# Long convolution of 1024 tokens: eight residues of 128 in place of four of 256, with the larger butterfly on VectorE

## The chip, the cores and the metric

One core of one Trainium2 chip runs the whole program. The metric is device time in microseconds; three runs of the kernel before gave 2500.44, 2504.18 and 2507.24, median 2504.18.

## The reference, cut to what matters

One encoder layer is applied to two groups with shared weights: "sample" (1024 tokens, group 0 in the kernel) and "prompt" (512 tokens, group 1). The part that changes is the Hyena branch's bidirectional long convolution over the sequence, for 512 channels:

```python
def bidir_long_conv(v, h_f, h_b):
    L = v.shape[1]
    k = concatenate([h_f, zeros, h_b[1:][::-1]])          # filter of length 2L
    return irfft(rfft(v, 2 * L) * rfft(k, 2 * L), 2 * L)[:, :L]
y = bidir_long_conv(v, h_f, h_b) + v * fbias
```

`h_f`, `h_b` come out of a small sine MLP, times a decaying window, divided by the sum of absolute values. After it come the branch projections, gates, an output projection, and a squared-ReLU MLP: `x + gt2 * (square(relu(h2 @ w_ff1)) @ w_ff2)`. All in float32; the kernel writes each operand of a matmul as a high and a low part (`fp32r`) and sums three products.

## The kernel before, in words

**Transform.** The convolution is done by matmuls against cosine and sine tables at odd frequencies, in groups ("units") of 128 channels, four units for each group of tokens. The sequence of length L is split into four residues (token index modulo 4) of L/4 each, so the sample has residues of 256 and the prompt of 128. `filter_spectrum` (L504) makes eight tap blocks with two matmuls of 256 columns each (L515 to L540), then the spectrum: for each of two frequency halves `j`, 24 matmuls of 128 columns for the even residues (L564, L565) and 24 of 256 columns for the odd ones (L578, L580), all through `dft_mm` (L496), combined on VectorE and stored to DRAM (`d_b`). `long_conv` (L598) transposes the input (L621), runs for each half `j` 24 matmuls of 256 columns (L634), a four-point butterfly, the product with the spectrum and the inverse butterfly on VectorE (L645 to L679), transposes back (L691), and at the end 48 matmuls of 256 columns to token order (L721). The tables are streamed from DRAM on POOL's queue, 1 MB at a time, into the ring `cst` (three buffers in the spectrum, two in the convolution; L485 to L494): ten loads of `k_fs` and four of `k_gs` for each unit.

**Order.** Spectrum and convolution of the sample are generators that run beside the main work: `run(main, bg, ratio)` (L1421) emits `ratio` steps of the background for each step of the main generator. For the sample (L1576 to L1595) the main work is the prompt's branch projections (8 steps, ratio 1), its output projection (8, ratio 1), one step of the sample's gate products, and the prompt's MLP `ffn` (L1027; 64 steps, ratio 2.0). Each `ffn` step is 24 matmuls of 512 columns, for one weight block of 512 KB that SP's queue loads and that is split into high and low parts on ACT (L196) and VectorE (L198). The "up" steps evacuate through ACT (relu, square) and VectorE (L1035 to L1039), the last of every four "down" steps through VectorE (`gated_add`, L971 and L972). The builder's scheduler then places instructions on each engine; it may put an instruction that is ready ahead of one emitted earlier. Engines run their instructions in that fixed order.

**After it.** `load_y` (L1594, L901) reads the convolved sample from `d_y` and splits it (L889, L890) for the sample's branch projections, which begin at once (L1627). PSUM has two banks for the background (`bg`) and four for the main matmuls in this stretch.

Of the kernel before, what the change touches and what calls it, by code (L numbers as in the profile page):

```python
# [12 lines left out]
F32 = mybir.dt.float32  # L13
# [8 lines left out]
P = 128  # L22
# [28 lines left out]

def _row_order(L):
    q = L // 4
    return np.concatenate([4 * np.arange(q) + r for r in range(4)])


def _constants():
# [15 lines left out]
    for L, tag in zip(LENS, "sp"):  # L73
        J = L // 4
        nj, nu = J // P, J // P
        om = math.pi * (np.arange(J) + 0.5) / L
        F = np.zeros((nj, P, 6, nu, 2, P))
        G = np.zeros((4, P, nj, 2, J))
        for r in range(4):
            ang = np.outer(om, 4.0 * np.arange(J) + r)  # L80
            for cs, fn in enumerate((np.cos, np.sin)):
                m = fn(ang)
                f = m.reshape(nj, P, nu, P).transpose(0, 3, 2, 1)
                slot = (r // 2) if r % 2 == 0 else 2 + r // 2
                F[:, :, slot, :, cs, :] = f
                if r % 2 == 1:
                    F[:, :, 4 + r // 2, :, cs, :] = -f if cs else f
                G[r, :, :, cs, :] = m.reshape(nj, P, J).transpose(1, 0, 2)
        c["k_f" + tag] = np.stack(_hilo(F), 3)
        c["k_g" + tag] = np.stack(_hilo(G), 2)  # L90
    i = np.arange(P)
    ms = [i[:, None] == i[None]]
# [17 lines left out]
def encoder_trunk(ctx: ExitStack, tc: tile.TileContext, a: dict, dbg=None):  # L110
# [374 lines left out]
    def load_f(pool, g, j, s0, bufs):  # L485
        t = pool.tile([P, 2, 2, n_of[g] // 512, 2, P], F32R, name="cst", bufs=bufs)
        G.dma_start(t, a["k_f" + tags[g]][j][:, s0:s0 + 2])
        return t

    def load_g(pool, g, r0, nb, bufs):  # L490
        n = n_of[g]
        t = pool.tile([P, nb, 2, n // 512, 2, n // 4], F32R, name="cst", bufs=bufs)
        G.dma_start(t, a["k_g" + tags[g]][r0:r0 + nb].rearrange("r p h j s u -> p r h j s u"))
        return t  # L494
# [9 lines left out]
    def filter_spectrum(g, u, h3, wo, pool):  # L504
        n = n_of[g]
        nu = n // 512
# [3 lines left out]
        F = load_f(pool, g, 0, 0, 3)  # L510
        pm = {}
        for r in range(4):
            for ut in range(nu):
                i = r * nu + ut
                ps = psum("bg")[:, 0:2 * P]  # L515
                T.matmul(ps, lhsT=h3[:, i * P:(i + 1) * P], rhs=wo[0][:, :, c0:c0 + P], start=True, stop=False)
                T.matmul(ps, lhsT=h3[:, i * P:(i + 1) * P], rhs=wo[1][:, :, c0:c0 + P], start=False, stop=True)
                win = pool.tile([P, P], F32, name="kwin", bufs=3)
                nc.sync.dma_start(win, a["k_win"][row0 + i * P:row0 + (i + 1) * P, c0:c0 + P])
                hw = pool.tile([P, 2, P], F32, name="khw", bufs=2)  # L520
                V.tensor_tensor(hw, ps.rearrange("p (d c) -> p d c", d=2),
                                win[:, None, :].broadcast_to([P, 2, P]), op=ALU.mult)
                hw2 = hw.rearrange("p d c -> p (d c)")
                if i == 0:
                    V.memset(hw[0:1, 1, :], 0.0)
                    S.activation(acc, hw2, AF.Abs)
                else:
                    ab = pool.tile([P, 2 * P], F32, name="kab", bufs=1)
                    S.activation(ab, hw2, AF.Abs)
                    V.tensor_tensor(acc, acc, ab, op=ALU.add)  # L530
                f = pool.tile([P, 2, P], F32, name="kpm", bufs=2)
                V.tensor_tensor(f[:, 0, :], hw[:, 0, :], hw[:, 1, :], op=ALU.add)
                s = (1, 0) if r == 3 else (0, 1)
                V.tensor_tensor(f[:, 1, :], hw[:, s[0], :], hw[:, s[1], :], op=ALU.subtract)
                fh = pool.tile([P, 2, P], F32R, name=f"kh{i}", bufs=1)
                S.copy(fh, f)
                fl = pool.tile([P, 2, P], F32R, name=f"kl{i}", bufs=1)
                V.tensor_tensor(fl, f, fh.bitcast(F32), op=ALU.subtract)
                pm[r, ut] = (fh, fl)
                yield  # L540
# [5 lines left out]
        V.reciprocal(nsc[:, g * 4 + u:g * 4 + u + 1], tmp)  # L546

        def terms(F, lst, cs):
            res = []
            for r, d, slot in lst:  # L550
                for ut in range(nu):
                    fh, fl = pm[r, ut]
                    res.append((fh[:, d, :], fl[:, d, :], F[:, slot, 0, ut, cs, :], F[:, slot, 1, ut, cs, :]))
            return res
# [3 lines left out]
        for j in range(n // 512):  # L558
            Fo = load_f(pool, g, j, 2, 3)
            Fn = load_f(pool, g, j, 4, 3)  # L560
            eb = []
            for r in (0, 2):
                ps = psum("bg")[:, 0:2 * P]
                dft_mm(ps[:, lo], terms(F, [(r, 0, r // 2)], C))  # L564
                dft_mm(ps[:, hi], terms(F, [(r, 1, r // 2)], Sn))  # L565
                eb.append(ps)
            s0 = pool.tile([P, 2 * P], F32, name="ks0", bufs=1)
            S.copy(s0, eb[0])
            e0 = pool.tile([P, 2 * P], F32, name="ke0", bufs=1)
            e1 = pool.tile([P, 2 * P], F32, name="ke1", bufs=1)  # L570
            V.tensor_tensor(e0, s0, eb[1], op=ALU.add)
            V.tensor_tensor(e1, s0, eb[1], op=ALU.subtract)
            if (j + 1) * 512 < n:
                F = load_f(pool, g, j + 1, 0, 3)
            yield
            yield
            pp = psum("bg")[:, 0:2 * P]
            dft_mm(pp, terms(Fo, [(1, 0, 0)], CS) + terms(Fn, [(3, 0, 1)], CS))  # L578
            mm = psum("bg")[:, 0:2 * P]
            dft_mm(mm, terms(Fn, [(1, 1, 0)], CS) + terms(Fo, [(3, 1, 1)], CS))  # L580
            Bt = pool.tile([P, 4, 2 * P], F32, name="kB", bufs=1)
            V.tensor_tensor(Bt[:, 0, lo], e0[:, lo], pp[:, lo], op=ALU.add)
            V.tensor_tensor(Bt[:, 2, lo], e0[:, lo], pp[:, lo], op=ALU.subtract)
            V.tensor_tensor(Bt[:, 1, lo], e1[:, lo], pp[:, hi], op=ALU.subtract)
            V.tensor_tensor(Bt[:, 3, lo], e1[:, lo], pp[:, hi], op=ALU.add)
            V.tensor_tensor(Bt[:, 0, hi], e0[:, hi], mm[:, hi], op=ALU.subtract)
            V.tensor_tensor(Bt[:, 2, hi], e0[:, hi], mm[:, hi], op=ALU.add)
            V.tensor_tensor(Bt[:, 1, hi], e1[:, hi], mm[:, lo], op=ALU.add)
            V.tensor_tensor(Bt[:, 3, hi], e1[:, hi], mm[:, lo], op=ALU.subtract)
            G.dma_start(d_b[g][u][j], Bt)  # L590
            yield
# [6 lines left out]
    def long_conv(g, u, pool, vx, ahead):  # L598
        n = n_of[g]
        nu = nj = n // 512  # L600
        J = n // 4
# [6 lines left out]
        def load_b(j):  # L608
            t = wt()
            nc.sync.dma_start(t, d_b[g][u][j])  # L610
            return t

        Fe = load_f(pool, g, 0, 0, 2)
        Bt = load_b(0)
        yield
        yield
        v = {}
        for r in range(4):
            ps = psum("bg")
            for ut in range(nu):  # L620
                T.transpose(ps[:, ut * P:(ut + 1) * P], _ap(vx, 4 * ut * P + r, [[4, P]]), ident)  # L621
            vh = pool.tile([P, nu, P], F32R, name=f"lvh{r}", bufs=1)
            pv = ps[:, 0:nu * P].rearrange("p (u c) -> p u c", u=nu)
            S.copy(vh, pv)
            vl = pool.tile([P, nu, P], F32R, name=f"lvl{r}", bufs=1)
            V.tensor_tensor(vl, pv, vh.bitcast(F32), op=ALU.subtract)
            for ut in range(nu):
                v[r, ut] = (vh[:, ut, :], vl[:, ut, :])
        Fo = load_f(pool, g, 0, 2, 2)
        yield  # L630

        def fwd(F, r):
            ps = psum("bg")[:, 0:w2]
            dft_mm(ps, [v[r, ut] + (F[:, r // 2, 0, ut, :, :], F[:, r // 2, 1, ut, :, :]) for ut in range(nu)])  # L634
            return ps

        nb = 1 if J == 256 else 4
        Q = []
        for j in range(nj):
            At = wt()  # L640
            tmp = wt()
            b0 = fwd(Fe, 0)
            S.copy(tmp[:, 0, :], b0)
# [1065 lines left out]
```

## Time and profile before

| | |
|---|---|
| median of 3 runs | 2504.18 us |
| profiled execution | 2507.51 us |
| its span, first to last instruction | 2505.7 us |
| mean granted TensorE clock (share of 2.4 GHz) | 0.989 |
| PE / PEld / DVE / ACT busy | 2445.6 / 2003.5 / 1722.4 / 996.1 us |
| POOL's DMA queue (q0), moved | 161.91 MB |

PE is the matmul engine, PEld its weight loads, DVE is VectorE, ACT is ScalarE, POOL is GpSimd, SP only issues DMAs. Matmuls are pipelined: a record covers a matmul's whole way through the array, so the cost of one in a stream is the distance from its start to the next start, not the length of its record. Idle times of an engine come with the instruction that ended them.

### The profile page before, as it was taken

To read this page: it belongs to the slowest core of one execution; us is meant where nothing else is said; L and a number is where in the kernel's file an instruction comes from. 1 tells how busy PE (TensorE), PEld (TensorE's weight loads), DVE (VectorE), ACT (ScalarE), POOL (GpSimd) and SP (SyncE) were. 2 spreads that over 40 slices of the span, in tenths; PEclk is the share of its full clock that TensorE was granted. 3 is DMA by queue.
4 is the path that set the end of the run, shared out by engine and by line. 5 is a ranking of instruction groups with operands and counts; after the bars stand their busy time and mean duration, and the time that the engine had idled before them with its cause. 6 is when DMAs were issued, how large, how long until landed. Compare 5 with 4: busy or idle time off the path is not lost.

```text
span 2505.7 us, 32508 instructions
## 1 busy us (share of the span) xinstructions
PE 2445.6 (98%) x11874; PEld 2003.5 (80%) x11874; DVE 1722.4 (69%) x3056; ACT 996.1 (40%) x1607; POOL 200.7 (8%) x353
## 2 busy tenths in 40 slices
PE   8999999999999999999999999999999999999998
PEld 3777888788887888878788888887887888788886
DVE  4876778876675858666666766677756787645556
ACT  4354465222234334343533322333446444433344
POOL 0000100112100000000000000000100111100100
PEclk9999999999999999999999999999999999999999
DMA  7336655668523323166667666658757665575554
GB/s 231 121 111 194 199 173 157 210 215 276 188 69 92 109 64 114 54 225 215 204 214 236 239 219 226 220 202 296 235 164 231 207 230 189 176 275 197 192 195 160
DMA packets 358648, 471.36 MB, mean 188 GB/s; under 512 B 19685, under 2 KB 242053, under 8 KB 351320
## 3 DMA queue, kind: packets, MB, share of 16 engines
q1 hardware_dynamic: 303896, 279.05, 35.7%
q0 software_dynamic: 39024, 161.91, 18.7%
q10 hardware_dynamic: 15568, 28.32, 3.1%
q8 instruction: 93, 1.52, 0.2%
q14 instruction: 67, 0.55, 0.1%
HBM read 374.42 MB, written 94.78 MB: 187 GB/s over the span
## 4 chain that ended last, share of the span: by engine, by line
PE 65%; issue 24%; DMA 5%; DVE 4%; ACT 1%; POOL 1%; SPq 0%; DVEq 0%; POOLq 0%; ACTq 0%
PE mm L1318 12%; PE mm L1088 12%; PE mm L219 7%; PE mm L218 7%; PE mm L220 7%; PE mm L965 4%; PE mm L967 4%; PE mm L966 4%; PE bg L501 3%; DMA arow<-ada_w 2%; PE bg L721 1%; PE aux L798 1%; DMA cst<-k_fs 1%; PE bg L691 0%; DMA kwin<-k_win 0%
## 5 line engine op out<-in xcount | busy, mean ns | idle before, releaser
L198 DVE TENSOR_TENSOR wl<-wf,wh 128x1024 fp32r<-128x1024 f32 (+1 forms) x246 | 297.2, 1210 | 348.6 <-ACT wh L196 348.3
L196 ACT CAST wh<-wf 128x1024 fp32r<-128x1024 f32 (+1 forms) x246 | 255.4, 1039 | 635.4 <-PE mm L219 352.8
L219 PE MATMUL mm<-hl,wh 128*128 128x512 f32 x1152 | 458.1, 398 | 0.0
L218 PE MATMUL mm<-hh,wh 128*128 128x512 f32 x1152 | 456.9, 397 | 0.0
L220 PE MATMUL mm<-hh,wl 128*128 128x512 f32 x1152 | 455.7, 396 | 0.0
L218 PEld LDWEIGHTS mm<-hh,wh 128*128 128x128 f32 x1152 | 217.6, 189 | 50.4 <-issue 4.8
L219 PEld LDWEIGHTS mm<-hl,wh 128*128 128x128 f32 x1152 | 217.7, 189 | 45.9 <-issue 2.4
L220 PEld LDWEIGHTS mm<-hh,wl 128*128 128x128 f32 x1152 | 217.7, 189 | 44.5 <-issue 0.8
L1318 PE MATMUL mm<-wh,Bh 128*128 128x512 f32 x448 | 175.4, 392 | 3.1 <-ACT Bh L1300 3.1
L1318 PE MATMUL mm<-wh,Bl 128*128 128x512 f32 x448 | 175.1, 391 | 1.6 <-DVE Bl L1302 1.6
L1318 PE MATMUL mm<-wl,Bh 128*128 128x512 f32 x448 | 175.2, 391 | 0.0
L1302 DVE TENSOR_TENSOR Bl<-af,Bh 128x1024 fp32r<-128x1024 f32 x56 | 68.2, 1224 | 119.1 <-ACT Bh L1300 119.0
L218 PE MATMUL mm<-Ah,wh 128*128 128x512 f32 x312 | 123.3, 398 | 5.4 <-ACT Ah L889 3.0
L219 PE MATMUL mm<-Al,wh 128*128 128x512 f32 x312 | 123.3, 396 | 1.4 <-DVE Al L890 1.4
L220 PE MATMUL mm<-Ah,wl 128*128 128x512 f32 x312 | 122.4, 393 | 0.0
L1300 ACT CAST Bh<-af 128x1024 fp32r<-128x1024 f32 x56 | 58.7, 1052 | 156.9 <-PE mm L1318 135.7
L1318 PEld LDWEIGHTS mm<-wh,Bh 128*128 128x128 f32 x448 | 84.6, 189 | 21.2 <-ACT Bh L1300 3.5
L1318 PEld LDWEIGHTS mm<-wh,Bl 128*128 128x128 f32 x448 | 84.6, 189 | 20.3 <-DVE Bl L1302 2.7
L965 PE MATMUL mm<-wh,Bh 128*128 128x512 f32 x256 | 100.4, 392 | 0.0
L967 PE MATMUL mm<-wh,Bl 128*128 128x512 f32 x256 | 100.1, 391 | 0.0
L966 PE MATMUL mm<-wl,Bh 128*128 128x512 f32 x256 | 100.0, 391 | 0.0
L1318 PEld LDWEIGHTS mm<-wl,Bh 128*128 128x128 f32 x448 | 84.7, 189 | 17.4
(429 smaller groups left out, 5160.3 us busy)
## 6 DMA issues: line engine op xcount, KB each, us to landing
wf<-w_ff SPq DMA_DIRECT2D x100, 512.0 KB
wf<-w_in SPq DMA_DIRECT2D x96, 512.0 KB
cst<-k_fs POOLq DMA_DIRECT2D x40, 1024.0 KB, 7.3
w<-w_ff SPq DMA_DIRECT2D x64, 256.0 KB
d_t<-w POOLq DMA_DIRECT2D x64, 256.0 KB, 5.5
arow<-ada_w SPq DMA_DIRECT2D x64, 256.0 KB
cst<-k_gs POOLq DMA_DIRECT2D x16, 1024.0 KB, 6.1
wq<-w_ff SPq DMA_DIRECT2D x32, 512.0 KB
```

Of the source, the lines that this page charges most:

```text
L196: S.copy(wh, wf)
L198: V.tensor_tensor(wl, wf, wh.bitcast(F32), op=ALU.subtract)
L218: T.matmul(ps, lhsT=wh[:, i, cs], rhs=ah, start=(i == 0), stop=False)
L219: T.matmul(ps, lhsT=wh[:, i, cs], rhs=al, start=False, stop=False)
L220: T.matmul(ps, lhsT=wl[:, i, cs], rhs=ah, start=False, stop=(i == n - 1))
L501: T.matmul(ps, lhsT=x, rhs=f, start=(i == 0), stop=(i == n - 1))
L965: T.matmul(ps, lhsT=ah[:, cs], rhs=wh[:, k, :], start=(first and k == 0), stop=False)
L966: T.matmul(ps, lhsT=ah[:, cs], rhs=wl[:, k, :], start=False, stop=False)
L967: T.matmul(ps, lhsT=al[:, cs], rhs=wh[:, k, :], start=False, stop=(last and k == n - 1))
L1088: T.matmul(ps, lhsT=w[:, i, :], rhs=x, start=(first and i == 0 and k == 0), stop=(last and i == n - 1 and k == 2), skip_group_check=True)
L1302: V.tensor_tensor(lo, t, hi.bitcast(F32), op=ALU.subtract)
L1318: T.matmul(pss[i], lhsT=x[:, n, cs], rhs=w[:, n, :], start=(first and k == 0 and n == 0 and m == 0), stop=(last and k == 7 and n == 1 and ...
```

## The change

The sample's sequence is split into eight residues (token index modulo 8) of 128, and all 128 frequencies of a residue are done in one go, so that the two halves `j` and the two halves of each residue are gone. What the four-point butterfly did is now an eight-point one on VectorE, with multiplications by the square root of one half on ACT. The prompt keeps four residues of 128 (its functions are renamed `spectrum4` and `conv4`, with the loops of length one taken out). The table ring holds three buffers of 768 KB in the spectrum and three of 512 KB in the convolution. In `ffn` the second squaring moves from VectorE to ACT. The background's ratio in `ffn` goes from 2.0 to 2.25. The tap part of the spectrum (now `filter_taps`) does what it did.

```diff
+HALF = float(np.float32(math.sqrt(0.5)))
+EIGHT = (0, 2, 1, 7, 4, 6, 5, 3)
+    def spectrum8(u, h3, wo, pool):
+        def table(k):
+            t = pool.tile([P, 2, 2, 3, P], F32R, name="cst", bufs=3)
...
+        F0, F2, F1 = table(0), table(2), table(1)
+        pm = yield from filter_taps(0, u, h3, wo, pool)
...
+        def pair(F, r):
+            ps = psum("bg")
+            dft_mm(ps[:, 0:2 * P], [term(F, r, 0, 0, slice(0, 2)), term(F, 8 - r, 1, 0, slice(0, 2))])
+            dft_mm(ps[:, 2 * P:], [term(F, r, 0, 1, slice(1, 3)), term(F, 8 - r, 1, 1, slice(1, 3))])
+            return ps
...
+        U, W, Dt = [pool.tile([P, 4, 2 * P], F32, name=nm, bufs=1) for nm in ("kU", "kW", "kD")]
+        ps = psum("bg")
+        for i, r in enumerate((0, 4)):
+            for d in range(2):
+                c0 = (2 * i + d) * P
+                dft_mm(ps[:, c0:c0 + P], [term(F0, r, i, d, slice(d, d + 1))])
+        S.copy(Dt[:, 0:2, :], ps.rearrange("p (k c) -> p k c", k=2))
+        F3 = table(3)
+        # two tensor_tensor of 256; yield; pair(F2, 2), four of 256; yield
+        # pair(F1, 1), copied by ACT; yield; pair(F3, 3), six of 256, one scaling by HALF on ACT; yield
+        V.tensor_tensor(W, U, Dt, op=ALU.add)
+        G.dma_start(d_b[0][u][0], W)
+        V.tensor_tensor(U, U, Dt, op=ALU.subtract)
+        G.dma_start(d_b[0][u][1], U)
+        yield
+    def turn_q(qh, ql, k, srcs):      # four transposes into one bank, split by ACT and VectorE
...
+    def back(ps, qh, ql, gt):
+        lst = []
+        for cs in range(2):
+            qs = slice(cs * P, (cs + 1) * P)
+            lst += [(qh[:, qs], gt[:, 0, cs, :]), (qh[:, qs], gt[:, 1, cs, :]), (ql[:, qs], gt[:, 0, cs, :])]
+        for k, (l, rh) in enumerate(lst):
+            T.matmul(ps, lhsT=l, rhs=rh, start=(k == 0), stop=(k == len(lst) - 1))
+    def conv8(u, pool, vx, ahead):
+        def table(k):
+            t = pool.tile([P, 2, 2, 2, P], F32R, name="cst", bufs=3)
+            G.dma_start(t, a["k_es"][:, 2 * k:2 * k + 2])
+            return t
+        es = [table(0), table(1)]
...
+        v = pool.tile([P, 8, w2], F32R, name="lq", bufs=2)
+        for r0 in (0, 4):             # four transposes, split into high and low; yield
...
+        es.append(table(2))
+        def fwd(r):
+            F = es.pop(0)
+            ps = psum("bg")
+            for i in range(2):
+                dft_mm(ps[:, i * w2:(i + 1) * w2], [(v[:, r + 2 * i, lo], v[:, r + 2 * i, hi], F[:, i, 0], F[:, i, 1])])
+            return ps.rearrange("p (k c) -> p k c", k=2)
+        X, Yt, A = wt(), wt(), wt()   # 128 x 2048 each
+        for k in range(2):
+            ks = slice(2 * k, 2 * k + 2)
+            S.copy(X[:, ks, :], fwd(k))
+            pb = fwd(4 + k)
+            tt(X[:, 4 + 2 * k:6 + 2 * k, :], X[:, ks, :], pb, 1)
+            tt(Yt[:, ks, :], X[:, ks, :], pb, -1)
+            if k == 0:
+                es.append(table(3))
+            yield
+        S.activation(Yt[:, 2:4, :], Yt[:, 2:4, :], AF.Copy, scale=HALF)
+        # butterfly: 2 tensor_tensor of 128, 1 of 256, 3 of 512; yield; 6 of 256, 2 of 512; yield
+        V.tensor_tensor(X, A, Bt, op=ALU.mult)
+        yield
+        V.tensor_tensor(av, av, _ap(Bt, P, [[w2, 8], [-P, 2], [1, P]]), op=ALU.mult)
+        yield
+        # 2 of 1024; yield; 2 of 1024; yield; 2 of 128, 3 of 256, 1 of 512 and HALF on ACT; yield
+        # 4 of 256; yield; 2 of 1024; yield; yield; four turn_q with a yield each
...
+        for r0 in (0, 4):
+            ps = psum("bg")
+            for i in range(4):
+                if i % 2 == 0:
+                    gt = gs.pop(0)
+                    yield
+                back(ps[:, i * P:(i + 1) * P], qh[:, r0 + i, :], ql[:, r0 + i, :], gt[:, i % 2])
+                if r0 == 0 and i == 1:
+                    gs.append(load_g(pool, 0, 6, 2, 3))
...
+        yield
+        V.tensor_tensor(y, y, x0, op=ALU.mult)
+        G.dma_start(d_y[0][u], y)
@@ ffn
-                S.activation(ah, r, AF.Square)
-                V.tensor_tensor(r, r, r, op=ALU.mult)
+                S.activation(r, r, AF.Square)
+                S.copy(ah, r)
                 V.tensor_tensor(al, r, ah.bitcast(F32), op=ALU.subtract)
@@ the sample's stage
-    run(up, bg, 2.0)
+    run(up, bg, 2.25)
```

(The lines that begin with `# ` after the plus sign stand for several lines of code.)

## Rows read from the trace of the kernel before

**Rows 1.** The page's busy times: engine, us, share, instructions.
```profile
PE 2445.6 (98%) x11874; PEld 2003.5 (80%) x11874; DVE 1722.4 (69%) x3056; ACT 996.1 (40%) x1607; POOL 200.7 (8%) x353
```

**Rows 2.** Stretches of the sample's stage: us, busy per engine, PEclk, DMA share, GB/s.
```profile
1310.00:1390.00 80.00, 80.00 (x453) 70.11 (x453) 48.32 (x116) 22.44 (x38) 7.99 (x15) 1.00 0.67 221
1465.00:1540.00 75.00, 75.00 (x388) 63.70 (x387) 54.05 (x95) 24.64 (x39) 5.06 (x10) 1.00 0.68 228
1110.00:1700.00 590.00, 580.20 (x2976) 490.30 (x2975) 403.00 (x811) 203.11 (x346) 36.70 (x69) 0.99 0.67 221
```

**Rows 3.** PE timeline: start us, record us, line, shape, count.
```profile
1475.38 0.39 PE L218 MATMUL mm<-Ah,wh 128*128 128x512 f32 x1
1475.85 0.32 PE L501 MATMUL bg<-cst,lvh 128*128 128x256 f32 x1
```

**Rows 4.** PE timeline: first and last start of three runs of matmuls.
```profile
1164.96 0.31 PE L501 MATMUL bg<-cst,kh 128*128 128x128 f32 x1
...
1167.56 0.27 PE L501 MATMUL bg<-cst,kh 128*128 128x128 f32 x1
1473.95 0.28 PE L501 MATMUL bg<-cst,lvh 128*128 128x256 f32 x1
...
1475.26 0.28 PE L501 MATMUL bg<-cst,lvh 128*128 128x256 f32 x1
1679.69 0.39 PE L967 MATMUL mm<-wh,Bl 128*128 128x512 f32 x1
...
1684.46 0.40 PE L967 MATMUL mm<-wh,Bl 128*128 128x512 f32 x1
```

**Rows 5.** DVE and ACT groups of the stage: line, shapes, count, busy us, mean ns.
```profile
L1038 DVE TENSOR_TENSOR tt<-tt 128x512 f32<-128x512 f32 x32 | 22.1, 690 | 0.1
L664 DVE TENSOR_TENSOR lw<-lw 128x256 f32<-128x256 f32 x32 | 13.5, 420 | 0.0
L723 DVE SCALAR_TENSOR_TENSOR lw<-bg,nsc,lw 128x256 f32<-128x256 f32 x16 | 10.7, 670 | 0.2
L726 DVE TENSOR_TENSOR lw<-lw 128x1024 f32<-128x1024 f32 x4 | 4.9, 1225 | 0.1
L654 DVE TENSOR_TENSOR lw<-lw,bg 128x128 f32<-128x128 f32 x8 | 2.2, 280 | 0.0
L889 ACT CAST Bh<-tt 128x512 fp32r<-128x512 f32 x16 | 9.1, 613 | 0.1
```

**Rows 6.** DVE timeline inside one butterfly of the convolution.
```profile
1408.70 1.22 DVE L198 TENSOR_TENSOR wl<-wf,wh 128x1024 fp32r<-128x1024 f32 x1
1409.83 0.69 DVE L668 TENSOR_TENSOR lw<-lw 128x512 f32<-128x512 f32 x1
1410.43 0.69 DVE L669 TENSOR_TENSOR lw<-lw 128x512 f32<-128x512 f32 x1
```

**Rows 7.** DMA issues, the prompt's table loads: count, KB each, median us to landing.
```profile
cst<-k_fp POOLq DMA_DIRECT2D x20, 512.0 KB, 6.3
```

**Rows 8.** PE's waits of the stage: us in total, times, longest.
```profile
PE bg L501 <- DMA cst<-k_fs: 1.0, 2, 0.8
```

**Rows 9.** The chain at the stage's end: start us, us, what.
```profile
1689.33 2.90 DMA d_y<-lw
1693.56 5.51 DMA tt<-d_y
```

**Rows 10.** PE timeline at the stage's end; in brackets the idle time and its releaser.
```profile
1688.57 0.97 PE L218 MATMUL mm<-Ah,wh 128*128 128x512 f32 x3 [2.29 <-ACT Ah L889]
1699.26 0.50 PE L218 MATMUL mm<-Ah,wh 128*128 128x512 f32 x1 [0.75 <-ACT Ah L889]
1702.07 0.50 PE L219 MATMUL mm<-Al,wh 128*128 128x512 f32 x1 [0.85 <-DVE Al L890]
1711.41 0.77 PE L218 MATMUL mm<-Ah,wh 128*128 128x512 f32 x1 [2.38 <-DVE gt L910]
```

**Rows 11.** The five us behind that last gap, columns as in Rows 2.
```profile
1710.00:1715.00 5.00, 3.59 (x9) 2.90 (x10) 3.86 (x7) 1.28 (x2) 0.00 (x0) 0.66 1.01 337
```

More of the change, by code (lines that the diff above doesn't have):

```diff
@@ L509, in filter_spectrum @@
         acc = pool.tile([P, 2 * P], F32, name="kacc", bufs=1)
[L510 to L540, printed above, removed]
@@ new lines, in filter_taps @@
+        pm = []
+        for i in range(R):
+            ps = psum("bg")[:, 0:2 * P]
+            T.matmul(ps, lhsT=h3[:, i * P:(i + 1) * P], rhs=wo[0][:, :, c0:c0 + P], start=True, stop=False)
+            T.matmul(ps, lhsT=h3[:, i * P:(i + 1) * P], rhs=wo[1][:, :, c0:c0 + P], start=False, stop=True)
+            win = pool.tile([P, P], F32, name="kwin", bufs=3)
+            nc.sync.dma_start(win, a["k_win"][row0 + i * P:row0 + (i + 1) * P, c0:c0 + P])
+            hw = pool.tile([P, 2, P], F32, name="khw", bufs=2)
+            V.tensor_tensor(hw, ps.rearrange("p (d c) -> p d c", d=2),
+                            win[:, None, :].broadcast_to([P, 2, P]), op=ALU.mult)
+            hw2 = hw.rearrange("p d c -> p (d c)")
+            if i == 0:
+                V.memset(hw[0:1, 1, :], 0.0)
+                S.activation(acc, hw2, AF.Abs)
+            else:
+                ab = pool.tile([P, 2 * P], F32, name="kab", bufs=1)
+                S.activation(ab, hw2, AF.Abs)
+                V.tensor_tensor(acc, acc, ab, op=ALU.add)
+            f = pool.tile([P, 2, P], F32, name="kpm", bufs=2)
+            V.tensor_tensor(f[:, 0, :], hw[:, 0, :], hw[:, 1, :], op=ALU.add)
+            s = (1, 0) if 2 * i > R else (0, 1)
+            V.tensor_tensor(f[:, 1, :], hw[:, s[0], :], hw[:, s[1], :], op=ALU.subtract)
+            fh = pool.tile([P, 2, P], F32R, name=f"kh{i}", bufs=1)
+            S.copy(fh, f)
+            fl = pool.tile([P, 2, P], F32R, name=f"kl{i}", bufs=1)
+            V.tensor_tensor(fl, f, fh.bitcast(F32), op=ALU.subtract)
+            pm.append((fh, fl))
+            yield
@@ L557, in filter_spectrum @@
         lo, hi = slice(0, P), slice(P, 2 * P)
[L558 to L591, printed above, removed]
@@ new lines, in spectrum4 @@
+        Fo = load_f(pool, 2, 3)
+        Fn = load_f(pool, 4, 3)
+        eb = []
+        for r in (0, 2):
+            ps = psum("bg")[:, 0:2 * P]
+            dft_mm(ps[:, lo], terms(F, [(r, 0, r // 2)], C))
+            dft_mm(ps[:, hi], terms(F, [(r, 1, r // 2)], Sn))
+            eb.append(ps)
+        s0 = pool.tile([P, 2 * P], F32, name="ks0", bufs=1)
+        S.copy(s0, eb[0])
+        e0 = pool.tile([P, 2 * P], F32, name="ke0", bufs=1)
+        e1 = pool.tile([P, 2 * P], F32, name="ke1", bufs=1)
@@ L596, in load_vx, with conv4 @@
         return vx
[L598 to L601, printed above, removed]
+    def conv4(u, pool, vx, ahead):
         w2 = 2 * P
@@ new lines, in conv4 @@
+            ahead.append(load_vx(1, u + 1, pool))
+        ps = psum("bg")
+        for i in range(4):
+            back(ps[:, i * P:(i + 1) * P], qh[:, i, :], ql[:, i, :], gs[:, i])
+        view = _ap(y, 0, [[1, 4], [4, P]])
+        V.scalar_tensor_tensor(view, ps.rearrange("p (r u) -> p r u", r=4), nsc[:, 4 + u:5 + u], view,
+                               op0=ALU.mult, op1=ALU.add)
+        yield
+        V.tensor_tensor(y, y, x0, op=ALU.mult)
+        G.dma_start(d_y[1][u], y)
+    def turn_q(qh, ql, k, srcs):
+        ps = psum("bg")
+        for i in range(4):
+            T.transpose(ps[:, i * P:(i + 1) * P], srcs[i // 2][:, (i % 2) * P:(i % 2 + 1) * P], ident)
+        pv = ps.rearrange("p (r c) -> p r c", r=2)
+        S.copy(qh[:, k:k + 2, :], pv)
+        V.tensor_tensor(ql[:, k:k + 2, :], pv, qh[:, k:k + 2, :].bitcast(F32), op=ALU.subtract)
@@ L1462, in convolve @@
         for u in range(4):
-            yield from long_conv(g, u, cv, ahead.pop(0), ahead)
+            yield from (conv8 if g == 0 else conv4)(u, cv, ahead.pop(0), ahead)
         closed(z_cv)
```

379 lines of the change are left out of this document (242 added, 137 removed).

## The prediction

> **What bounds the kernel now.** I read the page's busy times first. PE is busy 98% of the span, with DVE at 69% and ACT at 40% [rows 1], so the first guess is that PE's work sets the time. A busy record is no proof, so the second view is the sample's own stage, 1110 to 1690 us, cut into stretches: where the spectrum runs (1310 to 1390) and where the convolution runs (1465 to 1540) PE has no idle time at full clock, DVE is busy 60% and 72%, and the DMA engines stand at 0.67 and 0.68 [rows 2]. The third view is PE's timeline. When the background's next matmul isn't ready, the scheduler has put a main matmul before it, and the two kinds alternate with no gap [rows 3]. So in this stage a matmul taken away should be time taken away, as long as the rest is ready. Main and background work share one PE, and the stage ends when both are through.
>
> **Matmuls removed.** The cost of a matmul in a stream is its distance to the next start. From the first to the last start of each run [rows 4]: 24 matmuls of 128 columns take 2.60 us over 23 steps, 0.113 us; 12 of 256 columns take 1.31 us over 11 steps, 0.119 us; 22 main ones of 512 columns take 4.77 us over 21 steps, 0.227 us. Halving 256 columns to 128 buys nearly nothing; fewer matmuls buy all.
> Per unit, before: the spectrum has 48 of 128 columns and 48 of 256, the convolution 48 of 256 forward and 48 of 256 back: 48 x 0.113 + 144 x 0.119 = 22.6 us. After: the spectrum has 12 of 128 (F0) and 36 of 256 (three pairs), the convolution 24 of 256 forward (eight residues, three each) and 48 of 128 back (eight residues, six each): 60 x 0.113 + 60 x 0.119 = 13.9 us. The tap matmuls, 8 transposes in and 16 transposes out stay. Saved: 8.7 us a unit, 34.6 us for four units.
>
> **DVE.** Durations are 0.280, 0.420, 0.690 and 1.225 us for 128, 256, 512 and 1024 elements [rows 5]; the product over 2048 elements isn't there. From below it is 1.225, from above two of 1024, 2.45; the slope from 512 to 1024 gives 2.29, which I take.
> Spectrum, per unit: 4 of 256 and 16 of 128 (6.2 us) become 12 of 256 and 2 of 1024 (7.5 us), so +1.3. Convolution, per unit: the two half passes had, with the splits, 4 + 2 x 12 instructions of 256, 2 x 9 of 512 and 2 x 4 of 128, 26.4 us, and 4 evacuations of 0.670 [rows 5]. After: splits 2 x 0.69, forward 4 x 0.69, the first butterfly 7.0, products 4.6, sums 2 x 2.45, the inverse 2.5 + 1.7 + 2.45, splits 4 x 0.69, together 30.0, and two evacuations of 512. These are between 0.67 and 2 x 0.67 each; taken at the upper end they cost what they did. So +3.6. Four units: +20 us. The MLP's squaring leaves DVE: 32 x 0.690 = 22 us [rows 5]. DVE's sum changes by about -2 us, on 403 us of 590 [rows 2].
> ACT gets 32 copies of 512, 32 x 0.613 = 20 us [rows 5], and three scalings of 512 a unit, 7 us. It was busy 203 us of 590 [rows 2] and stays under half. The chain from a relu to the low part is still four instructions long, and its result is wanted only by the "down" steps behind it. I cost these edits at nothing on PE; without that cover the MLP copies would cost up to 20 us.
>
> **What may come late: the butterfly.** One unit's butterfly, from the scaling to the last sum before the transposes, lies on nine background steps. At 2.25 steps for a main step that is four main steps, 4 x 24 x 0.227 = 21.8 us of PE. On DVE it is 23.1 us by durations; but consecutive instructions of 512 start 0.60 apart and one of 1024 takes 1.13 [rows 6], which makes it 20.3 us. Beside it stand four weight splits of 1.13 and four low parts of 0.60, 6.9 us. DVE then needs 27.2 us in 21.8: it comes out 5.4 us late. Behind it wait the four output transposes, PSUM evacuations of the main matmuls and the weight splits, which are made two steps ahead. One empty background step (about 2.4 us of main matmuls) and the scheduler's reordering lie in between. So 0 to 5.4 us a unit, 0 to 21.6 us in all.
>
> **What may come late: the tables.** The convolution takes four tables in two consecutive steps out of a ring of three. The fourth can only be issued when the first is used up, 0.7 us into these steps. Table loads of 512 KB took 6.3 us to land [rows 7], plus 0.5 us of issue; one main step between the two is 5.4 us and the matmuls around it 1.4 us. So with a main step between it is just in time, and without one PE waits some 5 us. Counting steps, the four units' pairs fall with a main step between in three cases and without one in the last. In the stage before, PE waited for a table for 1.0 us in all [rows 8].
> By the Trainium skill, "DMA: Bandwidth & Descriptors", section "Anatomy of one DMA", a transfer issued by GpSimd takes about 2.0 us plus its bytes at 436 GB/s, which is an estimate of 3.2 us for 512 KB. With that no table would be late and the sum below would be some 3 us better. The trace doesn't agree in this stage: 6.3 us at the same size, with the DMA engines two thirds busy, and the sum goes by the trace.
> For the butterfly and the tables together I take 6 us, near the lower end (0 and 27), because the row nearest to them is the 1.0 us wait, and PE's order can be filled with main matmuls as it was.
>
> **The stage's end.** The background has 1 + 56 + 88 = 145 steps before (spectra 14 a unit, convolutions 22 a unit) and 1 + 52 + 100 = 153 after (13 and 25). The main work drives 1 + 17 + 64 x 2.0 = 146 of them before, so that the last `d_y` is issued at 1689.33, after the MLP, and its load into the next stage lands at 1699.07 [rows 9]. With 2.25 it drives 162 and the background ends four main steps, 22 us, earlier. PE's idle times behind the stage's end are 2.29, 0.75, 0.85 and 2.38 us [rows 10], and at the last the clock fell to a mean of 0.66 over five us [rows 11], (1 - 0.66) x 5 = 1.7 us more. The 0.75 and 0.85 wait for the late load and go. The other two are DVE's and ACT's backlog of evacuations and final normalisation, and may stay. Gain between 0 and 8.0, taken as 2.
>
> **Transfers.** Constants fall from fourteen 1 MB loads a unit to 2.75 MB plus 4 MB: about 29 MB less on POOL's queue. DMA isn't last on PE here, so no gain is counted.
>
> **Sum.** -34.6 + 6 - 2 = -30.6 us. From the profiled execution's 2507.5 (span 2505.7, 1.8 around it) that gives 2476.9; this execution lay 3.3 over the median 2504.2, so the forecast is 2473.6 us.
>
> **Rivals.**
> *Half given back.* DVE's lateness shows in full on PE: 4 x 5.4 = 21.6 us, and the gain at the end is nil: 2504.2 - 34.6 + 21.6 = 2491.2. For it: 72% of DVE in the convolution's stretch, and a burst twice as long as before. Against it: the old burst, half as long, left PE without idle time [rows 2].
> *More than the sum.* Nothing is late and all idle time at the stage's end goes: 2504.2 - 34.6 - 8.0 = 2461.6. For it: PE never waited here; against it: two of the four gaps aren't the convolution's.
> *The table ring, slower.* In each unit PE stands at the fourth table (6.8 - 0.7 = 6.1 us) and again at the next unit's first, if its load queues on POOL behind the store of `y`: the scheduler used to issue those loads first. That store waits 2.5 + 1.2 us for DVE, two issues and the landing make 7.3, against 6.4 us of main work: 4.6 us. After each such stand the clock is down as in [rows 11], 1.7 us twice. That is 14.1 us a unit, 56.4 in all: 2504.2 - 34.6 + 56.4 = 2526.0. It decides from 8.7 us a unit. Against it: the 1.0 us of [rows 8].
> *No change.* PE's records are full but the stage runs at the pace of its weight loads and splits; then fewer matmuls only open gaps: 2504. Against it: DMA and DVE both stand near 70% [rows 2].
>
> **How the numbers follow.** Forecast 0.60, half given back 0.23, more 0.06, table ring 0.05, no change 0.06. What this kernel can tell from no change is about 0.3%, 7.5 us. Faster by more: 0.60 + 0.06 + 0.22 of the half case = 0.88; within: 0.07; slower: 0.05. The range leaves out the slower case, no change and the far ends: 2460 to 2492.
>
> **What would show it.** PE has 4 x 72 = 288 matmuls less; the stage ends some 30 us earlier after the same start; PE's waits on the transposes of the convolution and on `cst` stay under 6 us; DVE's sum is within 10 us of before; no PE wait for the last `d_y`. Wrong it would be if PE shows new gaps of several us in each unit, released by DVE or by a table's DMA, or if the gain appears outside the stage.

## The result, and the profile after

The changed kernel takes 2475.47 us (median of 4 runs, 2472.03 to 2476.31), the kernel before 2504.55 us beside it (4 runs, 2500.44 to 2507.24): a ratio of 0.9883, 95% interval [0.9866, 0.9900], 29.1 us less. The forecast was 2473.6 us. The profiled execution took 2472.03 us, with a span of 2470.2 us.

The page's busy times after, and POOL's DMA queue (packets, MB, share of 16 engines):

```profile
PE 2403.1 (97%) x11586; PEld 1967.4 (80%) x11586; DVE 1728.3 (70%) x2944; ACT 1022.0 (41%) x1635; POOL 199.4 (8%) x345
...
q0 software_dynamic: 39920, 131.50, 15.9%
```

Against [rows 1], PE has 288 matmuls less, as many as were counted. DVE has 5.9 us more and ACT 25.9 us more; POOL's queue moved 30.4 MB less.

To place the time, the stage needs two marks that no run's start-up shifts. The first is POOL's last store of the prompt's hidden part ahead of the stage (`d_y<-yt`), the second is the first matmul of the sample's output projection behind it. The two marks in the timeline of the kernel before:

```profile
1089.71 0.54 POOL L877 DMA_DIRECT2D d_y<-yt  x1 [0.60 <-ACT yt L876]
...
1734.81 0.39 PE L965 MATMUL mm<-wh,Ah 128*128 128x512 f32 x1
```

And in the timeline of the changed kernel:

```profile
1085.39 0.54 POOL L1060 DMA_DIRECT2D d_y<-yt  x1 [0.61 <-ACT yt L1059]
...
1701.20 0.39 PE L1148 MATMUL mm<-wh,Ah 128*128 128x512 f32 x1
```

The stage was 1734.81 - 1089.71 = 645.1 us and is 615.8 us: 29.3 us less, which is the whole of the 29.1. The first mark differs by 4.3 us between the two executions before anything of the change has run, so the spans (35.5 us apart) say too much.

Between the marks, by stretches (us, PE busy and matmul records, PEclk, DMA share, GB/s): start, spectrum, convolution, end. Before:

```profile
1089.70:1115.00 25.30, 20.05 (x81) 0.85 0.95 335
1115.00:1390.00 275.00, 271.43 (x1411) 0.99 0.66 216
1390.00:1680.00 290.00, 288.95 (x1486) 1.00 0.67 226
1680.00:1734.80 54.80, 47.95 (x202) 0.97 0.80 255
```

After, with 1340 to 1368, where the spectrum hands over to the convolution, by itself:

```profile
1085.40:1110.70 25.30, 20.03 (x82) 0.90 0.86 290
1110.70:1340.00 229.30, 226.01 (x1114) 0.98 0.58 188
1340.00:1368.00 28.00, 21.99 (x103) 0.88 0.80 250
1368.00:1640.00 272.00, 268.70 (x1354) 1.00 0.55 169
1640.00:1701.20 61.20, 56.53 (x243) 0.97 0.87 286
```

PE's busy time goes from 628.4 to 593.3 us, 35.1 less. Its idle time goes from 16.7 to 22.5 us: nothing at the start, 2.0 more in the long stretches (4.6 to 3.3 + 3.3), 6.0 new at the handover, 2.2 less at the end. PE's waits of the stage in the changed kernel (us in total, times, longest) name them:

```profile
PE bg L524 <- DVE khw L529: 6.0, 4, 2.0
PE bg L802 <- DMA lvx<-d_vx: 5.2, 1, 5.2
PE mm L230 <- ACT Ah L1072: 4.4, 1, 4.4
PE bg L512 <- DMA cst<-k_es: 2.2, 3, 0.8
...
PE mm L1148 <- DVE tt L1154: 1.6, 1, 1.6
...
PE bg L767 <- DVE lw L817: 0.2, 1, 0.2
```

The butterfly (`lw`, awaited by the output transposes, L767) is late for 0.2 us and the tables for 2.2. The 1.6 us for `tt` are one gap at 1527.8 us, in the third unit's convolution, where the MLP's evacuation stands in DVE's queue. What the forecast had not named is `lvx`, the first unit's convolution input, 5.2 us. The timeline at that place, DMA issues first, then PE:

```profile
1345.14 1.61 POOL L789 DMA_DIRECT2D cst<-k_es  x3
1346.16 0.79 SPq L670 DMA_DIRECT2D lvx<-d_vx  x1
1347.06 1.59 SPq L795 DMA_DIRECT2D lw<-d_b  x2
...
1351.53 0.39 PE L231 MATMUL mm<-Al,wh 128*128 128x512 f32 x1
1357.14 1.97 PE L802 MATMUL bg<-ident,lvx 128*128 128x128 f32 x8 [5.22 <-DMA lvx<-d_vx]
...
1359.33 0.63 PE L230 MATMUL mm<-Ah,wh 128*128 128x512 f32 x1
1359.76 0.63 PE L231 MATMUL mm<-Al,wh 128*128 128x512 f32 x1
```

The load is issued with three tables and 1 MB of spectrum and is there 11.0 us later; PE has main matmuls for half of that. Behind the gap matmuls of 512 columns start 0.43 us apart where they took 0.227 [rows 4]: the lower of PE's two clock levels, 1.2 of 2.4 GHz. These are the gap and twice 5 us behind it (PE, PEld, DVE, ACT, POOL busy, then PEclk, DMA share, GB/s):

```profile
1346.00:1357.00 11.00, 5.92 (x27) 4.56 (x25) 2.61 (x3) 2.82 (x5) 0.75 (x2) 0.89 1.06 333
1357.00:1362.00 5.00, 4.86 (x20) 4.38 (x21) 1.38 (x2) 1.17 (x2) 0.00 (x0) 0.56 0.65 206
1362.00:1367.00 5.00, 4.21 (x26) 3.45 (x25) 2.93 (x4) 3.75 (x6) 1.97 (x3) 1.00 0.63 177
```

The DMA engines are full while the load is under way (share 1.06), and at a mean clock of 0.56 the next 5 us cost, as an estimate, (1 - 0.56) x 5 = 2.2 us more. In the kernel before the same load was issued at 1385.70 us and first used at 1395.27; PE was busy for the whole of these 9.6 us, where here it has work for 5.4, and the DMA share was 0.93.

```profile
1385.70 0.34 SPq L595 DMA_DIRECT2D lvx<-d_vx  x1
...
1395.27 0.63 PE L621 MATMUL bg<-ident,lvx 128*128 128x128 f32 x4
```

The stage's end, where [rows 9, 10] had a late store and four gaps: the last store, the load of it, and PE.

```profile
1637.64 0.57 POOL L910 DMA_DIRECT2D d_y<-lw  x1 [11.30 <-DVE lw L909]
...
1653.03 2.23 SPq L1084 DMA_DIRECT2D tt<-d_y  x4
...
1661.02 1.03 PE L230 MATMUL mm<-Ah,wh 128*128 128x512 f32 x3 [4.40 <-ACT Ah L1072]
```

The store comes 51.7 us earlier (47.4 counted from the first mark), but its load stands 15.4 us behind it, because it is emitted after the whole MLP. Four gaps have become one of 4.4 us with one of 0.3 behind it, and PE's idle time there is 2.2 us less.

### The profile page after: what moved, and what is told of

It reads as the page before. It is cut to its first block, busy times and chain, and to the rows that moved or that the text cites. A ratio compares the mean times of both kernels' runs of the same rounds, so it can differ in the third digit from the quotient of the medians.

```text
span 2470.2 us, 31815 instructions
## 1 busy us (share of the span) xinstructions
PE 2403.1 (97%) x11586; PEld 1967.4 (80%) x11586; DVE 1728.3 (70%) x2944; ACT 1022.0 (41%) x1635; POOL 199.4 (8%) x345
## 4 chain that ended last, share of the span: by engine, by line
PE 81%; issue 8%; DVE 6%; DMA 4%; ACT 1%; POOL 0%; SPq 0%; ACTq 0%; DVEq 0%; POOLq 0%
PE mm L1501 12%; PE mm L1271 12%; PE mm L231 12%; PE mm L230 11%; PE mm L232 11%; PE mm L1150 4%; PE mm L1148 4%; PE mm L1149 4%; PE aux L981 3%; DMA arow<-ada_w 2%; PE bg L512 2%; PE bg L778 1%; PE aux L1045 1%; PE aux L1023 1%; DMA cst<-k_es 1%
```

## The experiments

Twelve variants ran. Beside the times stands the length of the stage between the two marks, read in each variant's own trace; it leaves out what varies elsewhere (the first mark lay between 1084.7 and 1092.5 us). It is one execution each; two variants whose stages should hardly differ, the kernel before and E4, came out at 645.1 and 645.3. Over the first 25.3 us, where no edit has acted yet, PEclk was 0.85 in the kernel before and in E5 and 0.90 in the changed kernel, a difference of 1.3 us by itself. So differences near 2 us and under it are not built on alone.

| | median us (before beside it) | ratio to before | stage us | against the changed kernel's |
|---|---|---|---|---|
| changed kernel | 2475.47 (2504.55) | 0.9883 [0.9866, 0.9900] | 615.8 | |
| E1 convolution matmuls twice | 2505.39 (2504.12) | 1.0007 [0.9998, 1.0016] | 647.9 | +32.1 |
| E2 back matmuls 256 wide | 2474.70 (2502.89) | 0.9889 [0.9872, 0.9905] | 618.0 | +2.2 |
| E3 ratio 2.0 | 2485.61 (2504.12) | 0.9933 [0.9920, 0.9945] | 625.5 | +9.7 |
| E4 before, with the small edits | 2506.71 (2502.89) | 1.0014 [1.0005, 1.0024] | 645.3 | |
| E5 one product tripled | 2486.14 (2502.89) | 0.9939 [0.9924, 0.9954] | 626.8 | +11.0 |
| E6 squaring on DVE | 2473.71 (2504.12) | 0.9891 [0.9875, 0.9906] | 616.6 | +0.8 |
| E7 one product left out | 2470.82 (2504.03) | 0.9865 [0.9849, 0.9881] | 613.5 | -2.3 |
| E8 four table buffers | 2471.73 (2504.03) | 0.9871 [0.9856, 0.9886] | 614.4 | -1.4 |
| E9 input loaded early | 2469.01 (2502.89) | 0.9868 [0.9853, 0.9883] | 613.6 | -2.2 |
| E10 output loaded early | 2469.14 (2504.12) | 0.9863 [0.9849, 0.9876] | 611.1 | -4.7 |
| E11 both | 2469.52 (2504.03) | 0.9864 [0.9845, 0.9883] | 609.2 | -6.6 |
| E12 both, input issued later | 2464.04 (2505.07) | 0.9846 [0.9832, 0.9861] | 605.0 | -10.8 |

**E1: are the matmuls the gain?** Give back their number and nothing else.

```diff
-                dft_mm(ps[:, i * w2:(i + 1) * w2], [(v[:, r + 2 * i, lo], ...
+                for _ in range(2):
+                    dft_mm(ps[:, i * w2:(i + 1) * w2], [(v[:, r + 2 * i, lo], ...
-                back(ps[:, i * P:(i + 1) * P], qh[:, r0 + i, :], ql[:, r0 + i, :], gt[:, i % 2])
+                for _ in range(2):
+                    back(ps[:, i * P:(i + 1) * P], qh[:, r0 + i, :], ql[:, r0 + i, :], gt[:, i % 2])
```

> Every group of forward and backward matmuls of the sample's convolution is issued twice, the second time over the first (same result): 24 of 256 and 48 of 128 columns more a unit, 288 in all, the number that the change took away; DVE, ACT, the tables and all transfers stay. Theory (the gain is the matmuls, each at its distance in a stream): 4 x (24 x 0.119 + 48 x 0.113) = +33 us over the changed kernel, so about 4 us over the kernel before (ratio 1.0015), since 29 were gained in all. Rival 1 (the stage runs at the pace of DVE, of which two thirds of any extra work showed): PE's extra work fills time in which it would wait, +10 to +20. Rival 2 (the longer PE makes the tables and stores late): more than +40.

The stage is 32.1 us longer, against 33.1 by the price in a stream; the time is back at that of before. Both rivals fall: PE fills no idle time with the extra work, and nothing else becomes later. The smaller table loads stay in E1, so they are not where the gain came from. PE's whole page shows the count of [rows 1] again:

```profile
PE 2442.2 (97%) x11874; PEld 2003.4 (80%) x11874; DVE 1729.1 (69%) x2944; ACT 1023.0 (41%) x1635; POOL 199.4 (8%) x345
```

**E2: number or columns?** Back matmuls of 256 columns, as many as in the changed kernel (part of the output is overwritten).

```diff
-            lst += [(qh[:, qs], gt[:, 0, cs, :]), (qh[:, qs], gt[:, 1, cs, :]), (ql[:, qs], gt[:, 0, cs, :])]
+            ch = slice(0, 2) if wide else cs
+            lst += [(qh[:, qs], gt[:, 0, ch, :]), (qh[:, qs], gt[:, 1, ch, :]), (ql[:, qs], gt[:, 0, ch, :])]
-                back(ps[:, i * P:(i + 1) * P], ...
+                back(ps[:, w0:w0 + 2 * P], ..., True)
```

> The changed kernel with each of the 192 matmuls back to token order made 256 columns wide instead of 128; the sums of two residues overwrite one another, so that part of the output is left out. My theory: a matmul costs its start-to-start distance, 0.119 us against 0.113, so 192 x 0.006 = 1 us more than the changed kernel. Rival, cost by columns: 192 x 128 columns at 2.4 per ns, 10 us more.

The group of back matmuls, by line and shape (count, busy us, mean ns of a record), first in the changed kernel, then in E2:

```profile
L778 PE MATMUL bg<-cst,lq 128*128 128x128 f32 x192 | 22.3, 273 | 0.0
```

```profile
L779 PE MATMUL bg<-cst,lq 128*128 128x256 f32 x192 | 24.2, 282 | 0.0
```

Twice the columns cost 1.9 us over 192 matmuls, 0.010 each: the columns rival is out, and halving columns was worth next to nothing, as the forecast took it.

**E3: what is the ratio worth?**

```diff
-    run(up, bg, 2.25)
-    ya = load_y(0, 0, s3, range(8), "A")
+    run(up, bg, 2.0)
     finish(bg)
+    ya = load_y(0, 0, s3, range(8), "A")
```

> The changed kernel with 2.0 background steps for a main step, where it has 2.25, and the background ended before the load of its output. 153 background steps against 146 driven: the last seven run after the MLP with no main matmul beside them. Theory (the stage's end was worth about 2 us, and a background alone at the end leaves PE waiting for DVE and the store): +5 to +10 us over the changed kernel. Rival (DVE is the tight engine, and the slower pace gives the butterfly more room): 0 to -3.

9.7 us lost, as the theory had it. PE's timeline at the end (idle time and releaser in brackets): the background is left alone, and PE meets DVE, which has the prompt's last normalisations (`nn_v`) in its queue, then the fourth table, then the store's load.

```profile
1654.76 2.01 PE L767 MATMUL bg<-ident,lw 128*128 128x128 f32 x8 [4.92 <-DVE nn_v L191]
...
1664.37 2.40 PE L778 MATMUL bg<-cst,lq 128*128 128x128 f32 x12 [2.09 <-DMA cst<-k_gs]
1675.67 0.97 PE L230 MATMUL mm<-Ah,wh 128*128 128x512 f32 x3 [1.05 <-ACT Ah L1072]
```

Idle time is the smaller part of the loss: over the stage it is 25.3 us, 2.7 more than in the changed kernel. The same matmuls are busy for 7.0 us longer, and the stage's end shows where, at a mean clock of 0.86 against 0.97 (columns as in the stretches above):

```profile
1655.00:1714.00 59.00, 53.62 (x225) 0.86 0.75 240
```

**E4: the small edits alone, in the kernel before** (squaring on ACT, ratio 2.25):

```diff
-                S.activation(ah, r, AF.Square)
-                V.tensor_tensor(r, r, r, op=ALU.mult)
+                S.activation(r, r, AF.Square)
+                S.copy(ah, r)
-    run(up, bg, 2.0)
+    run(up, bg, 2.25)
```

> The kernel before with only the two small edits: the second squaring on ScalarE and the background ratio 2.25. My theory: the gain lies in the matmuls removed; here the background only ends some seven main steps earlier, 0 to 3 us less than the kernel before. Rival: the late load at the stage's end was the cost; 8 us less or more.

Not faster: 3.8 us slower by the times (1.0014, an interval above 1), though the stage is the same length to 0.2 us. The theory's 0 to -3 holds at most at its upper end, by the stage; the rival's -8 does not. Where the 3.8 us come from is open. Nothing of the 29 us comes from these edits by themselves; the ratio is needed only because the change adds eight background steps.

**E5: how near is the butterfly to being late?** The first product of each unit is computed three times over (same result), 4 x 2 x 2.29 = 18 us more of DVE.

```diff
-        V.tensor_tensor(X, A, Bt, op=ALU.mult)
+        for _ in range(3):
+            V.tensor_tensor(X, A, Bt, op=ALU.mult)
```

> The changed kernel with the first product of 2048 elements on VectorE done three times, some 4.5 us more VectorE work inside each unit's butterfly, 18 us in all. My theory: the butterfly's lateness is covered by the scheduler's reordering; at most 4 us more than the changed kernel. Rival, VectorE binds in the butterfly: the full 18 us more, so that only some 11 us are left of the gain over the kernel before.

A miss: 11.0 us of the 18 show. Two stretches of the convolution (columns as above), first of the changed kernel, then of E5:

```profile
1440.00:1510.00 70.00, 69.37 (x353) 58.48 (x352) 52.74 (x72) 30.59 (x45) 4.83 (x8) 1.00 0.58 177
1510.00:1580.00 70.00, 68.38 (x340) 57.45 (x339) 52.97 (x72) 20.11 (x28) 3.59 (x6) 1.00 0.54 166
```

```profile
1440.00:1510.00 70.00, 66.08 (x319) 54.69 (x318) 54.48 (x70) 28.08 (x42) 3.32 (x6) 0.98 0.49 158
1510.00:1580.00 70.00, 66.06 (x326) 55.37 (x326) 56.87 (x75) 17.52 (x24) 5.54 (x9) 0.98 0.56 173
```

PE's idle time rises from 0.6 and 1.6 us to 3.9 in each, while DVE stands at 78% and 81%. Its releasers on DVE, over E5's stage, are an evacuation of the MLP, the weight split and the butterfly (in the changed kernel 1.6, none and 0.2):

```profile
PE mm L1149 <- DVE tt L1155: 3.9, 2, 2.4
PE mm L232 <- DVE wl L210: 2.4, 1, 2.4
PE bg L767 <- DVE lw L817: 1.9, 2, 1.5
```

The four units are not alike. By the place of these waits in E5's timeline the first unit loses 0.5 us, the second 3.9, the third 3.9 (1.6 in the changed kernel) and the fourth none. So two units hide nearly all of the 4.6 us and two do not; why these two is not shown. And idle time is only 5.1 of the 11.0 us over the whole stage. The other 5.9 are longer busy time, and lower clock accounts for nearly all of it: 0.98 against 1.00 in the two stretches, (1 - 0.98) x 140 = 2.8 us as an estimate, and some 1.3 us each at the stage's start (0.85 against 0.90) and end (0.95 against 0.97). What stands at the start is not this edit's.

**E6: the same burden, spread.** About as much work on DVE as in E5, in every MLP step.

```diff
-                S.activation(r, r, AF.Square)
-                S.copy(ah, r)
+                S.activation(ah, r, AF.Square)
+                V.tensor_tensor(r, r, r, op=ALU.mult)
```

> The squaring of the MLP's relu goes back from ACT to DVE, and the high part is copied by ACT straight from it: 32 instructions of 512 elements, +22 us on DVE and as much off ACT, spread evenly over the whole MLP. Theory A (DVE is late only where the butterfly's burst stands; there the tripled product cost two thirds of its 18 us): the spread work is caught up between bursts, 0 to +5 us over the changed kernel. Theory B (DVE is the second bound of the whole stage): two thirds of 22 us, +12 to +18. Theory C (ACT's extra instruction sits in the chain to the down matmuls): faster, -2 to -5.

+0.8 us for 22 us of DVE: theory A. What E5 hit is then the burst and not DVE's sum. The edit also takes some 20 us of copies off ACT, so the 0.8 us are the net of both; no run burdens DVE alone and spread out.

**E7: was the butterfly late in the changed kernel?** The second product is left out, 9.2 us less of DVE (part of the computation is missing).

```diff
-        V.tensor_tensor(av, av, _ap(Bt, P, [[w2, 8], [-P, 2], [1, P]]), op=ALU.mult)
```

> The second of the two products of 2048 elements in each unit's butterfly is left out (part of the computation is missing): DVE has 4 x 2.3 = 9 us less, inside the burst, where two more such products a unit cost 12 us. Theory (the burst just fits: beyond its slack every us shows, below it none does): 0 to -1 us against the changed kernel. Rival (DVE sets the pace within the burst, and PE's order hides it): -5 to -6, two thirds of 9.

-2.3 us by the stage, between the two. By the times it is -4.7, near the rival's -5 to -6, but its interval overlaps the changed kernel's, so the times decide nothing here. The trace says what went: the wait for `tt` (1.6 us in the changed kernel) is gone and the tables' is 1.0 us shorter; the wait for `lw` is still 0.2 us. So the burst costs the changed kernel some 2 us of its stage, as far as one execution shows it, seen best in the evacuation that stands behind it on DVE; that is far less than the 21.6 us of the prediction's half case.

**E8: the table ring.**

```diff
-            t = pool.tile([P, 2, 2, 2, P], F32R, name="cst", bufs=3)
+            t = pool.tile([P, 2, 2, 2, P], F32R, name="cst", bufs=4)
```

> Four buffers of the convolution's tables instead of three, so that a unit's fourth load is issued a table earlier. In the changed kernel PE's waits for the tables came to 2.2 us. Theory (the ring of three is nearly enough): 0 to -2 us against the changed kernel. Rival 1 (tables hold PE back where the waits don't show it, as half clock behind them): -4 to -6. Rival 2 (loads issued earlier collide with the weight loads on the same DMA engines): +1 to +4.

-1.4 us: the theory. The waits for tables are gone, and the one for `lvx` is longer (5.2 before):

```profile
PE bg L802 <- DMA lvx<-d_vx: 6.8, 1, 6.8
```

With three buffers this wait lay between 3.9 and 5.8 us in the other variants that have it. Four table loads in place of three are issued just ahead of the input's, so the loads on POOL's queue and on SP's may get in each other's way. By the Trainium skill, "DMA: Bandwidth & Descriptors", section "Queues, rings and completion order", each DMA engine takes the queues that have work for it in turn, a packet at a time; the 6.8 us agree with that, and no run here separates it from other reasons.

**E9: the input loaded early**, in a pool of its own, since its place in the convolution's pool only comes free when the spectra end.

```diff
+    z_vx, vxp = opened("vx0", "right")
+    vx0.append(load_vx(0, 0, vxp))
     bg = chain(spectra(0, "right"), convolve(0))
...
-        ahead = [load_vx(g, 0, cv)]
+        ahead = [vx0.pop() if vx0 else load_vx(g, 0, cv)]
```

> The changed kernel with the convolution input of unit 0 loaded into a buffer of its own before the spectra, instead of at the convolution's start. My theory: the 5.2 us that PE stood waiting for this load, and the half clock behind it (some 2 us), go, so about 7 us less than the changed kernel, 36 us less than the kernel before. Rival: the wait is only the crowd of transfers at that point (1.5 MB of tables, 1 MB of spectrum); then the first table takes its place as the wait and 0 to 2 us are gained.

The wait for `lvx` is gone, yet the stage wins only 2.2 us of the theory's 7. That is near the rival's 0 to 2, but not for its reason: the waits for the tables grew by 1.0 us only. A new wait stands at the stage's start, where the load was put ahead of the spectra's weights on SP's queue (E9's waits):

```profile
PE bg L524 <- ACT woh L1630: 3.9, 1, 3.9
```

**E10: the output loaded early**, after 62 of the 64 MLP steps.

```diff
-    run(up, bg, 2.25)
-    ya = load_y(0, 0, s3, range(8), "A")
+    run(first(up, 62), bg, 2.25)
     finish(bg)
+    ya = load_y(0, 0, s3, range(8), "A")
+    finish(up)
```

> The load of the convolution's output for the next stage is issued after 62 of the 64 MLP steps, once the background is through, where it was issued after all of them. Theory (the change ends the background early but does not use it: in the changed kernel the last store was issued at 1637.6, the load of it at 1653.0, and PE then waits 4.4 us at a lower clock of 0.72): 4 to 6 us faster than the changed kernel, so about 34 under the kernel before. Rival (the wait is the backlog of evacuations and normalisation on DVE and ACT, not the load): 0 to -1.5 us.

The 4.4 us wait is gone and the stage is 4.7 us shorter: the theory; the load was the wait, not the backlog behind it. The longest of PE's waits from 1640 to 1700 us in E10 is now

```profile
PE mm L230 <- DVE tt L1154: 1.3, 1, 1.3
...
```

**E11: both repairs.**

> Both repairs together: unit 0's input of the convolution loaded in a pool of its own ahead of the spectra (alone 4.8 us under the changed kernel), and the load of the convolution's output issued after 62 of the 64 MLP steps (alone 6 us under it). Theory (two waits at different places, each its own): the gains add, 10 to 11 us under the changed kernel, ratio to the kernel before about 0.984. Rival (the waits share their cause, or the first shifts the background so that the second comes back): 5 to 7 us, ratio 0.986.

The theory missed: 10 to 11 us were expected, 6.0 came by the times and 6.6 by the stage, in the rival's range. The 10 to 11 had been added up from the two variants' times; the times don't show a sum (2469.52, like either alone), the stages do, 6.6 us against 2.2 + 4.7. The new wait of E9 is here again, 4.1 us.

**E12: both, with the input's load moved behind the first projection.**

```diff
     z_vx, vxp = opened("vx0", "right")
-    vx0.append(load_vx(0, 0, vxp))
...
     run(branch(1, 0, ws, ya, gate_p, s3, ms), bg, 1.0)
+    vx0.append(load_vx(0, 0, vxp))
```

> Both repairs, with unit 0's input still loaded ahead of the spectra, but issued after the first projection and no longer before the spectra's weights. In the kernel with both repairs the stage, from the last store of the prompt's part to the first projection of the sample's, is 609.2 us long (changed kernel 615.8), and PE waits 4.1 us for the spectra's weights at its start. Theory (that wait comes from the load put before the weights on SP's queue): it goes, and the stage is 605 to 607 us; the time 9 to 10 us under the changed kernel, ratio to the kernel before about 0.985. Rival (the start of the stage waits for the tap chain on DVE either way): 608 to 610 us, ratio 0.986.

The wait for the weights is gone and the stage is 605.0 us long, 4.2 less than in E11 and 10.8 less than in the changed kernel. At 2464.04 us the ratio to before, [0.9832, 0.9861], lies wholly under that of the changed kernel, [0.9866, 0.9900]: a version that beats both. The handover and the end in E12, columns as in the stretches above:

```profile
1340.00:1368.00 28.00, 25.42 (x126) 1.00 0.97 297
...
1630.00:1691.00 61.00, 59.77 (x263) 1.00 0.82 276
```

PE is idle 2.6 and 1.2 us there, where it was 6.0 and 4.7, and the clock stays at 1.00. From E10 to E12 the input's repair is worth 611.1 - 605.0 = 6.1 us, the order of the 5.2 us wait with the 2.2 us of lower clock behind it.

## Why the prediction was right, step by step

**Matmuls, -34.6.** Right: PE is busy 35.1 us less in the stage (the lower clock behind the gap included), and E1 gives back 32.1 of 33.1. By the Trainium skill, "TensorE: Matmul & The Clock Gate", section "Back-to-back issue gap", matmuls of 128 columns with their weight loads follow each other about 81 ns apart. The traces don't agree: it is 0.113 us here [rows 4]. Why is open; no run varies the operands' type.

**What comes late, +6.** The size is near, its place was not. Ahead of the stage's end PE's idle time rose by 8.0 us (2.0 in the long stretches, 6.0 at the handover). The term was put together from the butterfly and the tables; in the changed kernel these account for 0.2, 1.6 (`tt`) and 2.2 us, and the tables had cost 1.0 before. The bulk is the wait of 5.2 us for the first unit's input, with some 2.2 us of lower clock behind it. The step that failed is the list of what the convolution waits for: the load of `lvx` was in the code, with two background steps between it and its use, and no term was made for it. Without that wait the time would have been some 6 us lower (E12 against E10) and the forecast 4 us too high, so its closeness is partly luck. Of the signs in "what would show it", the bound of 6 us held for the output transposes and the tables, 2.4 us in all; with the input transposes, which the words do not exclude, it is 7.6. "No PE wait for the last `d_y`" did not hold (4.4 us, gone in E10), and DVE's sum, taken 2 us lower, rose by 5.9.

**The butterfly.** The working had DVE 5.4 us late in each unit and trusted one empty step and the scheduler to hide it. They do, nearly: E7 finds some 2 us in all, and in E5 two units of four have no room for two more products. That "half given back" was the next likeliest case was fair: two more products a unit and over a third of the gain is gone. The durations behind it held: the product of 2048 elements takes 2.289 us (2.29 taken), the evacuation of 512 took 1.217 (up to 1.34 taken).

```profile
L906 DVE SCALAR_TENSOR_TENSOR lw<-bg,nsc,lw 128x512 f32<-128x512 f32 x8 | 9.7, 1217 | 0.9 <-PE bg L778 0.9
L849 DVE TENSOR_TENSOR lw<-lw 128x2048 f32<-128x2048 f32 x4 | 9.2, 2289 | 0.1
```

**The tables.** The estimate of a stand of some 5 us where no main step lies between was too dark: loads of `k_es` landed in 5.4 us and of `k_gs` in 5.2 (6.3 taken), PE's longest wait for `k_es` was 0.8 us, and it waited for no `k_gs` at all. The table-ring rival falls with it. The row taken was not from this stage: the loads of [rows 7] are the prompt's, issued between 182 and 615 us, and the last line below, from the kernel before, has the sample's own convolution tables, twice the size, landing in less. First the changed kernel, then the kernel before:

```profile
cst<-k_es POOLq DMA_DIRECT2D x16, 512.0 KB, 5.4
cst<-k_gs POOLq DMA_DIRECT2D x16, 512.0 KB, 5.2
```

```profile
cst<-k_gs POOLq DMA_DIRECT2D x16, 1024.0 KB, 6.1
```

**Edits costed at nothing.** Right as far as shown: the squaring costs about the same on either engine (E6: +0.8).

**The stage's end, -2.** Right in size (idle 6.9 to 4.7 us), wrong in the picture: the early background does not bring the load forward, since that is emitted behind the MLP. The two short gaps went, and one of 4.4 us came, which goes with an earlier load (E10); the working had put the two long gaps down to DVE's and ACT's backlog. At the old ratio the stage would have been 9.7 us longer (E3), a loss avoided rather than a gain.

**Transfers.** Right: POOL's queue moved 30.4 MB less, and E1, which keeps that, is back at the time of before.

**"No change".** Refuted by E1: the stage moves with PE's matmuls nearly one for one.

## What to carry to other kernels

Where PE has no idle time, price a change by the number of its matmuls and their start-to-start distance, not by columns: 128 and 256 columns cost nearly the same here (0.113 and 0.119 us), 512 twice as much (0.227). For each piece of work that moves, list every load that it waits for and what PE has to do between issue and use; a buffer whose place comes free only when the stage before ends is the one to look at. Ending background work early pays only if the load that uses its result is issued early too, and a load that is moved forward may delay what stood behind it on its queue.

## What the runs showed that was not expected

A wait cost more than itself here. Behind the 5.2 us for `lvx` the granted clock stood at 0.56 over 5 us, with full speed after; and in E3 and E5, where the stage grew by 9.7 and 11.0 us with the same matmuls, idle time grew by only 2.7 and 5.1 us, and PE's busy time, at lower clock, by 7.0 and 5.9. DVE at 76% of a stretch (52.97 of 70 us) already held PE up for 1.6 us, and extra work in the burst showed in two units of four, while 22 us spread over the MLP, and taken off ACT, cost 0.8. Two repairs that the times could not tell from one (2469.0 to 2469.5 us for each and for both) were told apart by the length of the stage, 613.6, 611.1 and 609.2 us.
